# Rounding the attention and out-projection weights quarter by quarter from one queue

## The chip, the cores and the metric

The kernel runs on one core of a Trainium2 chip. The time is that of the device for one execution, in microseconds (us), the median of several runs. The engines are TensorE (PE in the rows; its weight loads are PEld), VectorE (DVE), ScalarE (ACT), GpSimd (POOL) and SyncE (SP), which issues almost all transfers (DMA). Every engine works through a queue of its own in order; engines wait for one another by semaphores.

## The reference: one hybrid decoder layer

The input is x, 1024 tokens of 1024 numbers, float32. In short:

```
h    = rms_norm(x, norm1_w)
proj = h @ w_in             # q, k, v of 4 attention heads; q, k, v, z, a, b of 4 DeltaNet heads
da_o = diff_attention(rms_norm(q), rms_norm(k), v, lam)    # (softmax(q1 k1^T) - lam softmax(q2 k2^T)) v, causal
da_o = rms_norm(da_o) * (1 - lam_init)
dn_o = gated_delta_rule(...)                               # in chunks of 64, from a causal convolution
x    = x + concat(da_o, dn_o) @ w_out                      # out-projection, 1024 x 1024
h    = rms_norm(x, norm2_w)
x    = x + relu(h @ w_up)^2 @ w_down                       # 1024 x 4096 and 4096 x 1024
```

## The kernel before

Every matrix operand is split into a rounded high part, made on ScalarE by a copy into the type fp32r, and a low part, the rest, subtracted on VectorE. A product is then three matmuls: high by high, low by high, high by low. For the normed activations the parts are `hH` and `hL`; for weights they are `wH` and `wL`, made from a raw tile `wraw` that a DMA fills.

The order of TensorE's instructions is fixed by a planner, the class `Interleave` (object `flow`). The parts of the kernel are generators ("streams") with a priority: a stream yields the planned time at which it may go on, and the planner, which keeps a clock of TensorE's planned work (`flow.now`) and planned queues of the other engines (`flow.chain`), takes the next ready stream and emits its instructions. The instructions of ScalarE, VectorE and SyncE are ordered behind that by a scheduler that goes by their emission order and what they depend on. So a planned time that is too early leads to an instruction that waits at the head of its engine's queue.

The stretch that matters here runs, in the profile, from about 300 to 670 us. In it work these streams, side by side:

- `da_units` (L802): six units, namely k, q and v of two head pairs. A unit is 256 columns of `w_in` for all 8 token tiles: 8 tiles of 24 matmuls of 128x256 (L824 to L826), each followed by a copy `qn` and, for q and k, a norm.
- `da_turns` (L781) transposes the normed q and k (L789, L790) and stores them in DRAM as `qa`, `qb` (`qk_d`).
- `scores` (L894) loads them back, multiplies (L944, L945, L947), takes the maximum (L949) and the exponential `pexp` (L953). `values` (L969) transposes the weights of attention (L980), copies them with ScalarE (`at`, L982), multiplies them with v (L992), copies the result (`om`, L997) and stores it (`mixa_d`).
- `mixed` (L1040) loads the mixed outputs back and turns them into `hH`, `hL` (`to_hT`, L239 to L245).
- `outproj` (L1065) multiplies by `w_out` in halves (L1079 to L1081), adds into `acc` (L1086), and begins the second norm in `norm2` (squares L1098, `nrt` L231, `nr` L232 on GpSimd, products `hn` L1105).
- `backs` (L1204) transposes the normed tiles (`turn_b`, L1181, L1182) and forms the operands of the MLP (`kept`, `T0h`, `T0l`, `hH`, `hL`), and `up_first` (L1257) does the first up-projection products (L1249 to L1251). The MLP uses a scheme of seven half-size products instead of eight; its weights go through `split` (L1166, copy L1168 and subtract L1169).

A unit's weights are four quarters of 256 KB. `load_unit` (L186) emits, for all four at once, the DMA (L198), the copy (L200) and the subtract (L201). There are only two buffers of `wraw`, so that quarters 3 and 4 can be loaded only after the subtracts of quarters 1 and 2. `da_units` and `outproj` call it when the unit before begins; `first_ops` (L1230) does likewise for the first up-projection weights, its second half emitted behind a product of the second norm (`normed_by`). `unit_time` (L656) gives the planned times at which the quarters are ready, by which the streams yield.

Of the kernel before, what the change touches and what calls it, by code (L numbers as in the profile page):

```python
# [18 lines left out]
P = 128  # L19
SEQ = 1024  # L20
DM = 1024
KB = DM // P
# [99 lines left out]
def tile_hymba_layer(  # L122
# [111 lines left out]
    def to_hT(src, tb, bank, k0=0, nk=KB, keep=None):  # L234
        sl = slice(tb * P, (tb + 1) * P)
        for g in range(0, nk, 4):
            ps = bank()
            for j in range(4):
                T.transpose(ps[:, j * P:(j + 1) * P], src[:, (g + j) * P:(g + j + 1) * P], ident)  # L239
# [4 lines left out]
            S.copy(hH[:, ks, sl], psv)  # L244
            V.tensor_tensor(hL[:, ks, sl], psv, hH[:, ks, sl].bitcast(F32), ALU.subtract)  # L245

    def normed(dst, src, wb, pool, parts=1):
        sq = pool.tile([P, DM], F32, tag="nsq", name="nsq", bufs=1)
# [407 lines left out]
    def unit_time(eng="V", rate=610.0):  # L656
# [3 lines left out]
            done.append(flow.chain(("S", 520.0), (eng, rate), start=start + DMA_T))  # L660
        return done

    def scan():
        St = {}
        psA = pA.tile([P, 512], F32, name="ps_A")
        PA = {h: psA[:, h * P:(h + 1) * P] for h in range(HEADS)}

        def load(c):
            pka = sb.tile([P, HEADS, 3, P], F32, tag="pka", name="pka", bufs=2)
            for h in range(HEADS):  # L670
                nc.sync.dma_start(pka[:, h], park_d[h, c, :, 0:3, :])
            return pka

        nxt = load(0)
        for c in range(NT):
# [126 lines left out]
    def da_units():  # L802
        todo = [(g, kind) for g in range(2) for kind in (1, 0, 2)]

        def unit_w(i):
            g, kind = todo[i]
            return load_unit(w_in_v, [(512 * kind + 256 * g, 256)]), unit_time()

        w = unit_w(0)
        freed = [0.0, 0.0]  # L810
        n = 0
        for i, (g, kind) in enumerate(todo):
            (wh, wl), wt = w
            for tb in range(NT):
                if tb == 0:
                    if i + 1 < len(todo):
                        w = unit_w(i + 1)
                    else:
                        pre.append((load_unit(w_out_v, [(0, 512)], 4, 4), unit_time()))
                sl = slice(tb * P, (tb + 1) * P)  # L820
                yield max(freed[n % 2], wt[0] if tb == 0 else 0.0), None
                ps = pj.tile([P, 512], F32, tag="pj", name="ps_qk")
                for k in range(KB):
                    T.matmul(ps[:, :256], hH[:, k, sl], wh[:, k, :], start=(k == 0), stop=False)  # L824
# [2 lines left out]
                    if k % 2 == 1:  # L827
                        flow.pe(6 * TR)
                        if k < KB - 1:
                            yield wt[k // 2 + 1], None  # L830
                while len(late) > 2:
                    yield flow.now + 50, None
                qn = sd.tile([P, 256], F32, tag="qn", name="qn", bufs=4)
                if kind == 2:
                    S.copy(qn, ps[:, :256])
# [4 lines left out]
                else:  # L840
                    sq = sd.tile([P, 256], F32, tag="qsq", name="qsq", bufs=1)
                    S.activation(sq, ps[:, :256], AF.Square)
                    S.copy(qn, ps[:, :256])
# [125 lines left out]
    def values():  # L969
        for _ in order:  # L970
# [4 lines left out]
            for g in range(0, tb + 1, 4):  # L975
# [3 lines left out]
                for j in range(ng):  # L979
                    T.transpose(pt[:, j * P:(j + 1) * P], pe[:, (g + j) * P:(g + j + 1) * P], ident)  # L980
                at = ap.tile([P, 512], F32, tag="at", name="at", bufs=2)
                S.copy(at[:, :ng * P], pt[:, :ng * P])  # L982
                ats.append(at)
                if g + 4 > tb:
                    ready.pop(0)
# [27 lines left out]

    def turn(src, t, tb, k0, keep=None):
        r = yield from flow.bank("px", at=t)
        to_hT(src, tb, lambda: bank_tile(px, r, "ps_tr"), k0, 4, keep)
# [48 lines left out]
    def outproj():  # L1065
# [5 lines left out]

        def half(kh, w, n, tb):
            sl = slice(tb * P, (tb + 1) * P)
            (wh, wl), wt = w
            r = yield from flow.bank("pf", at=wt[0])
            ps = bank_tile(pf, r, "ps_op")
            for k in range(4):
                kk = 4 * kh + k
# [2 lines left out]
                T.matmul(ps, hL[:, kk, sl], wh[:, k, :], start=False, stop=(k == 3))  # L1081
                flow.pe(648)
                if k < 3:
                    yield wt[k + 1], None
            a = accs[tb][:, 512 * n:512 * n + 512]
            V.tensor_tensor(a, a, ps, ALU.add)  # L1086
            t = flow.chain(vec(512))
# [3 lines left out]
        def norm2(tb, pos):  # L1091
# [10 lines left out]
            for i in range(2):  # L1102
                sl = slice(512 * i, 512 * i + 512)
                if i == 0 or pos >= 4:
                    normed_by[:] = [V.scalar_tensor_tensor(hn[i], accs[tb][:, sl], r, w2b[:, sl], ALU.mult, ALU.mult)]  # L1105
# [31 lines left out]
        while todo:  # L1137
# [22 lines left out]
            [P, 2, 512], F32, name="X1")  # L1160
        state["out"] = True

    normed_by, normed_at, held_back, banks, normed2, raws, kept, u, ups = [], {}, [], {}, set(), [], {}, {}, {}
    k1, k2, tok1, tok2 = slice(0, 4), slice(4, 8), slice(512, 1024), slice(0, 512)

    def split(dst, src):  # L1166
# [8 lines left out]
    def turn_b(hn, t, tb):  # L1175
        sl = slice(tb * P, (tb + 1) * P)
        for i in range(2):
            r = yield from flow.bank("px", at=t)
            p = bank_tile(px, r, "ps_tr")
            for j in range(4):  # L1180
                T.transpose(p[:, j * P:(j + 1) * P], hn[i][:, j * P:(j + 1) * P], ident)  # L1181
            S.copy(hn[i], p)  # L1182
            flow.pe(4 * TR)
            t = flow.chain(act(512))
            flow.hold(r, t)
# [43 lines left out]

    def first_ops(g):  # L1230

        ops = []
        for tag, ks in (("wH", k1), (("wL", "wH")[g], k2)):
            o = staged(tag)
            o = o[:, :2048].rearrange("p (a k c) -> p a k c", a=2, k=4)
            for p in range(2):
                raw = laid("wraw")[:, :512]
                raw = raw.rearrange("p (k c) -> p k c", k=4)
                cs = slice(p * P, p * P + P)
                nc.sync.dma_start(raw, w_up_v[:, ks, 512 * g + p * P:512 * g + p * P + P])  # L1240
                split((o[:, 0, :, cs], o[:, 1, :, cs]), raw)
            ops.append((o[:, 0], o[:, 1]))
        return ops

    def prod_up(ps, op, p, h, start, stop):

# [10 lines left out]
    def up_first():  # L1257
        while not state["free"] or len([d for d in normed_at if d < 4]) < 4 or "wu" not in pools:
            yield flow.now + 50, None
        wu, wt = pools["wu"]  # L1260
        yield max(normed_at[d] for d in range(4)), None
        for g in range(2):
            for i in range(2):
# [6 lines left out]
                        yield flow.now + 50, None  # L1270
                    bank = banks["Z"] = [bank_tile(px, ("px", p), f"Z{p}") for p in range(2)]
                for p in range(2):
                    yield wt[2 * i + p], None
                    for k in prod_up(bank[p], wu[i], p, H_OPS[i + 1], True, i == 1):
                        flow.pe(680)
                        if k < 3:
                            yield flow.now, None
                    if (g, i, p) == (0, 1, 0):
                        while not state["out"]:
                            yield flow.now + 50, None  # L1280
                        with tc.issue_after(normed_by[0].ins):
                            ahead = first_ops(1), unit_time()
            if g == 0:
                wu, wt = ahead

    def read_first():
        a0 = pools["uz"].tile([P, 2, 512], F32, tag="ua0", name="ua0")
# [335 lines left out]
```

## Time and profile before

| | |
|---|---|
| median of 3 runs | 1273.77 us (1269.63 to 1275.3) |
| the profiled execution | 1275.89 us, its span 1274.2 us |
| TensorE busy | 1230.6 us (97%) |
| VectorE, ScalarE, GpSimd busy | 827.6 us (65%), 596.8 us (47%), 146.2 us (11%) |
| mean granted TensorE clock | 0.992 |

In the rows that follow, a line such as L200 is a line of the kernel before; `x72` counts instructions; a bracket `[4.23 <-DMA wraw]` gives the idle time of that engine just before the instruction and what ended it. PEclk is the granted clock of TensorE as a share of the full one.

### The profile page before, as it was taken

The page shows a single profiled execution, that of the slowest core. Times are in us where ns is not written, and L with a number is a line of the kernel's source. Part 1 is how long each engine was busy: PE and PEld are TensorE (multiplying, and loading weights), DVE is VectorE, ACT ScalarE, POOL GpSimd, SP SyncE. Part 2 cuts the span into 40 slices and gives each one's busy share as a digit, 9 for nine tenths or more (in the row PEclk, how much of TensorE's full clock was granted, in tenths as well). Part 3 has the DMA queues.
Part 4 walks back from the last instruction along what each step waited for, and adds up shares of the span by engine and source line. Part 5 has one row for each costly group of instructions (what it writes and reads, how often), then busy time and mean ns, then how long its engine had stood idle before and what let it go on. Part 6 is the DMA issues. An engine that isn't in the chain of part 4 may idle for free.

```text
span 1274.2 us, 18904 instructions
## 1 busy us (share of the span) xinstructions
PE 1230.6 (97%) x6925; PEld 1061.7 (83%) x6925; DVE 827.6 (65%) x1412; ACT 596.8 (47%) x1173; POOL 146.2 (11%) x178
## 2 busy tenths in 40 slices
PE   6989999999998999999999999999999999999998
PEld 5968788899998997887788888888887788888887
DVE  6459888657646647776588656555566765677553
ACT  5335554334445545566567445544554333333331
POOL 2327411012212210001210000000000000000000
PEclk9989999999999999999999999999999999999999
DMA  7134464357849556433353645343368955422311
GB/s 251 41 83 122 115 177 125 89 182 221 281 144 248 159 170 178 96 95 107 122 182 129 218 166 178 136 164 127 122 215 304 356 198 195 169 99 100 122 44 67
DMA packets 165958, 200.55 MB, mean 157 GB/s; under 512 B 20921, under 2 KB 126185, under 8 KB 165865
## 3 DMA queue, kind: packets, MB, share of 16 engines
q1 hardware_dynamic: 165864, 199.34, 48.4%
q8 instruction: 55, 0.90, 0.3%
q14 instruction: 39, 0.31, 0.1%
HBM read 133.23 MB, written 66.06 MB: 156 GB/s over the span
## 4 chain that ended last, share of the span: by engine, by line
PE 84%; DMA 6%; DVE 5%; ACT 2%; issue 2%; SPq 1%; DVEq 0%; POOL 0%; ACTq 0%
PE X L1251 4%; PE X L1249 4%; PE X L1250 4%; PE X L1545 4%; PE X L1546 4%; PE X L1544 4%; PE ps_qk L824 3%; PE ps_qk L825 3%; PE ps_qk L826 3%; PE Y L1251 2%; PE Y L1249 2%; PE Y L1250 2%; DMA wraw<-in_w_in_dram 2%; PE ps_dn L206 2%; PE ps_o L992 2%; PE ps_dn L207 2%
## 5 line engine op out<-in xcount | busy, mean ns | idle before, releaser
L1168 ACT CAST hH<-ur 128x1024 fp32r<-128x1024 f32 x56 | 58.7, 1050 | 174.9 <-PE Z L1545 84.0
L1169 DVE TENSOR_TENSOR hL<-ur,hH 128x1024 fp32r<-128x1024 f32 x56 | 68.3, 1223 | 84.0 <-ACT hH L1168 84.0
L824 PE MATMUL ps_qk<-wH,hH 128*128 128x256 f32 x384 | 116.0, 302 | 0.0
L825 PE MATMUL ps_qk<-wL,hH 128*128 128x256 f32 x384 | 109.5, 285 | 0.0
L826 PE MATMUL ps_qk<-wH,hL 128*128 128x256 f32 x384 | 109.4, 285 | 0.0
L1169 DVE TENSOR_TENSOR op<-raw,op 128x1024 fp32r<-128x1024 f32 x48 | 58.7, 1223 | 74.2 <-PE X L1250 39.5
L1545 PE MATMUL X<-hL,hH 128*128 128x512 f32 x224 | 87.3, 390 | 2.1 <-DVE hL L1169 2.1
L1544 PE MATMUL X<-hH 128*128 128x512 f32 x224 | 87.3, 390 | 1.4 <-DVE b L1446 1.4
L1546 PE MATMUL X<-hH,hL 128*128 128x512 f32 x224 | 87.2, 389 | 0.0
L206 PE MATMUL ps_dn<-hH,wH 128*128 128x512 f32 x192 | 77.0, 401 | 4.9 <-ACT cp L441 4.9
L207 PE MATMUL ps_dn<-hL,wH 128*128 128x512 f32 x192 | 76.4, 398 | 0.0
L208 PE MATMUL ps_dn<-hH,wL 128*128 128x512 f32 x192 | 76.2, 397 | 0.0
L824 PEld LDWEIGHTS ps_qk<-wH,hH 128*128 128x128 f32 x384 | 74.5, 194 | 0.1
L825 PEld LDWEIGHTS ps_qk<-wL,hH 128*128 128x128 f32 x384 | 74.6, 194 | 0.0
L826 PEld LDWEIGHTS ps_qk<-wH,hL 128*128 128x128 f32 x384 | 74.2, 193 | 0.0
L201 DVE TENSOR_TENSOR wL<-wraw,wH 128x512 fp32r<-128x512 f32 (+1 forms) x72 | 50.4, 715 | 30.0 <-ACT wH L200 29.8
L200 ACT CAST wH<-wraw 128x512 fp32r<-128x512 f32 (+1 forms) x72 | 42.9, 620 | 57.3 <-DMA wraw<-in_w_in_dram 41.8
L1169 DVE TENSOR_TENSOR hL<-dw,hH 128x1024 fp32r<-128x1024 f32 x56 | 67.9, 1218 | 2.6 <-ACT hH L1168 2.6
L1168 ACT CAST op<-raw 128x1024 fp32r<-128x1024 f32 x48 | 50.4, 1052 | 36.9 <-PE Y L1251 19.9
L445 DVE SCALAR_TENSOR_TENSOR cy<-cp,pv,cy 128x512 f32<-128x512 f32 x72 | 59.4, 827 | 9.6 <-ACT cy L443 8.9
L1168 ACT CAST hH<-dw 128x1024 fp32r<-128x1024 f32 x56 | 58.4, 1047 | 12.4 <-PE Z L1546 8.1
L949 DVE TENSOR_REDUCE mx<-ps_sc 128x1 f32<-128x128 f32 (+7 forms) x64 | 47.7, 755 | 17.2 <-PE ps_sc L947 16.8
(340 smaller groups left out, 3457.8 us busy)
## 6 DMA issues: line engine op xcount, KB each, us to landing
ur<-ud SPq DMA_DIRECT2D x28, 1024.0 KB, 4.9
raw<-in_w_up_dram SPq DMA_DIRECT2D x32, 512.0 KB, 3.8
dw<-in_w_down_dram SPq DMA_DIRECT2D x32, 512.0 KB, 6.8
wraw<-in_w_in_dram SPq DMA_DIRECT2D x48, 256.0 KB, 3.2
qk_d<-qa SPq DMA_DIRECT2D x32, 256.0 KB, 3.6
ud<-ua SPq DMA_DIRECT2D x16, 512.0 KB, 4.2
ud<-s SPq DMA_DIRECT2D x16, 512.0 KB, 2.8
pka<-park_d SPq DMA_DIRECT2D x32, 192.0 KB, 4.2
```

What stands on the lines that cost most here:

```text
L206: T.matmul(ps, lh(k), rh(k), start=(k == 0), stop=False)
L207: T.matmul(ps, lh(k), rl(k), start=False, stop=False)
L824: T.matmul(ps[:, :256], hH[:, k, sl], wh[:, k, :], start=(k == 0), stop=False)
L825: T.matmul(ps[:, :256], hH[:, k, sl], wl[:, k, :], start=False, stop=False)
L826: T.matmul(ps[:, :256], hL[:, k, sl], wh[:, k, :], start=False, stop=(k == KB - 1))
L1168: S.copy(dst[0], src)
L1169: V.tensor_tensor(dst[1], src, dst[0].bitcast(F32), ALU.subtract)
L1249: T.matmul(ps, op[0][:, k, cs], h[0][:, k, :], start=start and k == 0, stop=False, skip_group_check=True)
L1250: T.matmul(ps, op[0][:, k, cs], h[1][:, k, :], start=False, stop=False, skip_group_check=True)
L1544: T.matmul(bank[t], v[0][:, j, sl], v[2][:, j], start=s0, stop=False, skip_group_check=True)
L1545: T.matmul(bank[t], v[0][:, j, sl], v[3][:, j], start=False, stop=False, skip_group_check=True)
L1546: T.matmul(bank[t], v[1][:, j, sl], v[2][:, j], start=False, stop=s1, skip_group_check=True)
```

## The change

The roundings of these weights are emitted by a stream of their own, `casts`, from one queue `wq`, a quarter at a time. A load is emitted by `load_part`: two at the start of the queue, and from then on one with each rounding that is emitted, if a unit with quarters left is queued. A quarter is due when the planner's clock has gone 300 ns beyond the assumed time of a load, `DMA_T` (2500 ns), from the load's emission; its copy is then emitted with an ordering edge behind the last ScalarE operation emitted (`state["act"]`, noted at the copies `qn`, `at`, `turn_b` and those of `to_hT`). The users wait by `part(w, i)`, quarter by quarter. `first_ops` returns a queue entry; its roundings may go on from the state "ready" or "out", and are no longer behind a product of the second norm.

```diff
+    def load_part(w):
+        i = len(w["raw"])
+        src, k = w["parts"][i][2:]
+        raw = laid("wraw")[:, :k * src.shape[-1]].rearrange("p (k c) -> p k c", k=k)
+        nc.sync.dma_start(raw, src)
+        w["raw"].append(raw)
+        w["due"].append(flow.now + DMA_T + 300.0)
+
+    def casts():
+        while "wu" not in pools or wq:
+            w = wq[0] if wq else None
+            if w is None or w["due"][len(w["at"])] > flow.now or not state.get(w["gate"], True):
+                yield flow.now + 50, None
+                continue
+            i = len(w["at"])
+            hi, lo = w["parts"][i][:2] if w["gate"] is None else w["ops"]()[i]
+            with tc.issue_after(state["act"].ins) if "act" in state else ExitStack():
+                S.copy(hi, w["raw"][i])
+            V.tensor_tensor(lo, w["raw"][i], hi.bitcast(F32), ALU.subtract)
+            w["at"].append(flow.chain(("S", 520.0), ("V", 610.0)))
+            if i == 3:
+                wq.pop(0)
+
+            nxt = next((v for v in wq if len(v["raw"]) < 4), None)
+            if nxt is not None:
+                load_part(nxt)
+            yield flow.now, None
+
+    def part(w, i):
+
+        while len(w["at"]) <= i:
+            yield flow.now + 50, None
+        yield w["at"][i], None
...
-            (wh, wl), wt = w
+            this, (wh, wl) = w, w["ops"]
             for tb in range(NT):
+                sl = slice(tb * P, (tb + 1) * P)
+                yield freed[n % 2], None
+                yield from part(this, 0)
                 if tb == 0:
-                    if i + 1 < len(todo):
-                        w = unit_w(i + 1)
-                    else:
-                        pre.append((load_unit(w_out_v, [(0, 512)], 4, 4), unit_time()))
-                sl = slice(tb * P, (tb + 1) * P)
-                yield max(freed[n % 2], wt[0] if tb == 0 else 0.0), None
+                    w = ahead_unit(*(unit_w(i + 1) if i + 1 < len(todo) else (w_out_v, [(0, 512)], 4, 4)))
+                    if i + 1 == len(todo):
+                        pre.append(w)
...
-                            yield wt[k // 2 + 1], None
+                            yield from part(this, k // 2 + 1)
...
-                S.copy(at[:, :ng * P], pt[:, :ng * P])
+                state["act"] = S.copy(at[:, :ng * P], pt[:, :ng * P])
...
-                    normed_by[:] = [V.scalar_tensor_tensor(hn[i], accs[tb][:, sl], r, w2b[:, sl], ALU.mult, ALU.mult)]
+                    V.scalar_tensor_tensor(hn[i], accs[tb][:, sl], r, w2b[:, sl], ALU.mult, ALU.mult)
...
-        w1 = load_unit(w_out_v, [(512, 512)], 4, 4), unit_time()
+        w1 = ahead_unit(w_out_v, [(512, 512)], 4, 4)
...
-            w = load_unit(w_out_v, [(512 * n, 512)], 0, 4), unit_time()
+            w = ahead_unit(w_out_v, [(512 * n, 512)], 0, 4)
...
-                    pools["wu"] = first_ops(0), unit_time()
+                    pools["wu"] = [first_ops(g) for g in range(2)]
...
-                    if (g, i, p) == (0, 1, 0):
-                        while not state["out"]:
-                            yield flow.now + 50, None
-                        with tc.issue_after(normed_by[0].ins):
-                            ahead = first_ops(1), unit_time()
-            if g == 0:
-                wu, wt = ahead
+            wu = pools["wu"][1]
...
+    flow.add(0.5, casts())
```

`ahead_unit` makes the tiles `wH`, `wL` and the list of four quarters, and `queued` puts them on the queue. The out-projection's `half` and `up_first` change their waits to `part` in the same way. Where a first-operand quarter lies depends on `halves`, which allots the tiles of the second half only when its first rounding is emitted.

More of the change, by code (lines that the diff above doesn't have):

```diff
@@ L243, in to_hT @@
                 S.copy(keep, psv)
-            S.copy(hH[:, ks, sl], psv)
+            last = S.copy(hH[:, ks, sl], psv)
             V.tensor_tensor(hL[:, ks, sl], psv, hH[:, ks, sl].bitcast(F32), ALU.subtract)
+        return last
     def normed(dst, src, wb, pool, parts=1):
@@ L661, in unit_time, with ahead_unit, queued @@
         return done
+    wq = []
+    def ahead_unit(src, ranges, k0=0, nk=KB):
+        width = sum(n for _, n in ranges)
+        st = 2 * UC // width
+        wh, wl = [staged(t)[:, :nk * width].rearrange("p (k c) -> p k c", k=nk) for t in ("wH", "wL")]
+        c0 = ranges[0][0]
+        parts = [(wh[:, k:k + st], wl[:, k:k + st], src[:, k0 + k:k0 + k + st, c0:c0 + width], st)
+                 for k in range(0, nk, st)]
+        return queued((wh, wl), parts)
+    def queued(ops, parts, gate=None):
+        w = {"ops": ops, "parts": parts, "gate": gate, "raw": [], "due": [], "at": []}
+        wq.append(w)
+        if len(wq) == 1:
+            load_part(w)
+            load_part(w)
+        return w
+    def load_part(w):
[27 more added lines that the diff above has]
+        yield w["at"][i], None
     def scan():
@@ L806, in unit_w @@
             g, kind = todo[i]
-            return load_unit(w_in_v, [(512 * kind + 256 * g, 256)]), unit_time()
-        w = unit_w(0)
+            return w_in_v, [(512 * kind + 256 * g, 256)]
+        w = {"ops": load_unit(*unit_w(0)), "at": unit_time()}
         freed = [0.0, 0.0]
@@ L834, in da_units @@
                 if kind == 2:
-                    S.copy(qn, ps[:, :256])
+                    state["act"] = S.copy(qn, ps[:, :256])
                     st = nc.sync.dma_start(v_d[g, tb], qn.rearrange("p (h e) -> p h e", h=2))
@@ L842, in da_units @@
                     S.activation(sq, ps[:, :256], AF.Square)
-                    S.copy(qn, ps[:, :256])
+                    state["act"] = S.copy(qn, ps[:, :256])
                     sn = sd.tile([P, 4], F32, tag="sn", name="sn", bufs=2)
@@ L1015, in turn @@
         r = yield from flow.bank("px", at=t)
-        to_hT(src, tb, lambda: bank_tile(px, r, "ps_tr"), k0, 4, keep)
+        state["act"] = to_hT(src, tb, lambda: bank_tile(px, r, "ps_tr"), k0, 4, keep)
         flow.pe(4 * TR)
@@ L1073, in half @@
             sl = slice(tb * P, (tb + 1) * P)
-            (wh, wl), wt = w
-            r = yield from flow.bank("pf", at=wt[0])
+            wh, wl = w["ops"]
+            yield from part(w, 0)
+            r = yield from flow.bank("pf")
             ps = bank_tile(pf, r, "ps_op")
@@ L1083, in half @@
                 if k < 3:
-                    yield wt[k + 1], None
+                    yield from part(w, k + 1)
             a = accs[tb][:, 512 * n:512 * n + 512]
@@ L1161, in outproj @@
         state["out"] = True
-    normed_by, normed_at, held_back, banks, normed2, raws, kept, u, ups = [], {}, [], {}, set(), [], {}, {}, {}
+    normed_at, held_back, banks, normed2, raws, kept, u, ups = {}, [], {}, set(), [], {}, {}, {}
     k1, k2, tok1, tok2 = slice(0, 4), slice(4, 8), slice(512, 1024), slice(0, 512)
@@ L1181, in turn_b @@
                 T.transpose(p[:, j * P:(j + 1) * P], hn[i][:, j * P:(j + 1) * P], ident)
-            S.copy(hn[i], p)
+            state["act"] = S.copy(hn[i], p)
             flow.pe(4 * TR)
@@ L1230, in first_ops, with halves @@
     def first_ops(g):
+        srcs = [w_up_v[:, ks, 512 * g + p * P:512 * g + p * P + P] for ks in (k1, k2) for p in range(2)]
         ops = []
[L1233 to L1243, printed above, removed]
+        def halves():
+            if not ops:
+                for tag in ("wH", ("wL", "wH")[g]):
+                    o = staged(tag)[:, :2048].rearrange("p (a k c) -> p a k c", a=2, k=4)
+                    ops.append((o[:, 0], o[:, 1]))
+            return [(o[0][:, :, p * P:p * P + P], o[1][:, :, p * P:p * P + P]) for o in ops for p in range(2)]
+        if g == 0:
+            halves()
+        w = queued(halves, [(None, None, src, 4) for src in srcs], ("ready", "out")[g])
+        w["halves"] = ops
+        return w
     def prod_up(ps, op, p, h, start, stop):
@@ L1259, in up_first @@
             yield flow.now + 50, None
-        wu, wt = pools["wu"]
+        wu = pools["wu"][0]
         yield max(normed_at[d] for d in range(4)), None
@@ L1272, in up_first @@
                 for p in range(2):
-                    yield wt[2 * i + p], None
-                    for k in prod_up(bank[p], wu[i], p, H_OPS[i + 1], True, i == 1):
+                    yield from part(wu, 2 * i + p)
+                    for k in prod_up(bank[p], wu["halves"][i], p, H_OPS[i + 1], True, i == 1):
                         flow.pe(680)
```

## The prediction

> **What bounds the kernel now.** I read the summary first, then TensorE's waits over the stretch whose order the change moves (300 to 700 us), then the rows of the rounding copies and the timelines around the two longest waits.
>
> ```profile
> span 1274.2 us, 18904 instructions
> PE 1230.6 (97%) x6925; PEld 1061.7 (83%) x6925; DVE 827.6 (65%) x1412; ACT 596.8 (47%) x1173; POOL 146.2 (11%) x178
> PE 84%; DMA 6%; DVE 5%; ACT 2%; issue 2%; SPq 1%; DVEq 0%; POOL 0%; ACTq 0%
> L200 ACT CAST wH<-wraw 128x512 fp32r<-128x512 f32 (+1 forms) x72 | 42.9, 620 | 57.3 <-DMA wraw<-in_w_in_dram 41.8
> ```
>
> TensorE is busy in 97% of the span, so what a change of order can bring is idle time and lost clock of TensorE, nothing else. The copy that rounds a weight quarter (L200) costs 0.62 us, and ScalarE stands idle ahead of these copies mostly for the load of the raw weights. ScalarE is busy 47% and can afford to wait; what it must not do is wait with somebody's work behind it. The waits of TensorE in the moved stretch:
>
> ```profile
> PE ps_qkt L789 <- ACT at L982: 3.7, 1, 3.7
> PE ps_tr L239 <- DMA mt<-mixa_d: 2.3, 2, 1.4
> PE ps_at L980 <- ACT om L997: 2.2, 1, 2.2
> PE ps_at L980 <- DVE hL L245: 1.5, 1, 1.5
> PE ps_sc L945 <- DMA qb<-qk_d: 1.3, 1, 1.3
> PE ps_o L992 <- ACT at L982: 1.0, 1, 1.0
> PE ps_qkt L789 <- DVE qn L849: 0.9, 1, 0.9
> PE ps_sc L944 <- ACT pexp L953: 0.8, 1, 0.8
> PE ps_qkt L789 <- ACT om L997: 0.7, 1, 0.7
> PE ps_qkt L789 <- ACT osq L745: 0.2, 1, 0.2
> ```
>
> The columns are us in total, times, longest. None names a weight, but the timeline of ScalarE shows what stood ahead of the named copies (start, duration, and in brackets the idle time before and its releaser):
>
> ```profile
> 409.35 0.20 ACT L953 ACTIVATION_READ_ACCUMULATOR pexp<-ps_sc,mx 128x1 f32 x1
> 413.78 0.62 ACT L200 CAST wH<-wraw 128x512 fp32r<-128x512 f32 x1 [4.23 <-DMA wraw<-in_w_in_dram]
> 414.31 0.26 ACT L982 COPY at<-ps_at 128x128 f32<-128x128 f32 x1
> ...
> 541.27 0.62 ACT L200 CAST wH<-wraw 128x512 fp32r<-128x512 f32 x1 [2.74 <-DMA wraw<-in_w_out_dram]
> 542.68 0.25 ACT L997 COPY om<-ps_o 128x128 f32<-128x128 f32 x1
> ```
>
> The third quarter's rounding waits 4.23 us for its load at the head of ScalarE's in-order queue, and the attention copy that TensorE wants stands behind it. Over the stretch:
>
> ```profile
> DMA wraw<-in_w_in_dram: 15.2, 7
> DMA wraw<-in_w_out_dram: 8.8, 4
> ```
>
> ScalarE waited eleven times, 24 us, at these copies; eight TensorE waits stand behind such a copy or the subtract after it, 3.7 + 2.2 + 1.5 + 1.0 + 0.9 + 0.8 + 0.7 + 0.2 = 11.0 us. The cause is that a unit's four loads and roundings are emitted together and only two raw buffers exist, so loads 3 and 4 start after subtracts 1 and 2, while their copies already stand in ScalarE's queue.
>
> **What the stalls cost beside their length.** TensorE's timeline and the table by windows (PE, PEld, DVE, ACT, POOL busy, then PEclk):
>
> ```profile
> 414.62 0.47 PE L789 MATMUL ps_qkt<-ident,qn 128*128 128x128 f32 x1 [3.75 <-ACT at L982]
> 415.32 0.41 PE L825 MATMUL ps_qk<-wL,hH 128*128 128x256 f32 x1
> 415.53 0.41 PE L826 MATMUL ps_qk<-wH,hL 128*128 128x256 f32 x1
> ...
> 415.00:420.00 5.00, 5.00 (x26) 5.00 (x25) 3.29 (x9) 1.99 (x6) 1.01 (x1) 0.51 0.61 176
> 540.00:545.00 5.00, 2.75 (x12) 1.96 (x11) 2.45 (x3) 3.43 (x9) 0.00 (x0) 0.78 0.48 136
> 545.00:550.00 5.00, 5.00 (x23) 4.12 (x23) 3.67 (x9) 1.97 (x4) 0.55 (x1) 0.88 0.36 103
> ```
>
> After the gap of 3.75 us the granted clock is 0.51 for 5 us: 5 x 0.49 = 2.4 us lost. After that of 2.25 us the loss is 5 x 0.22 + 5 x 0.12 = 1.7 us. No other gap of the stretch shows a dip, the longest of them 1.5 us. Together 4.1 us.
>
> [...]
>
> **The change, part by part.** No engine gets more instructions; copies, subtracts and loads change places between about 300 and 670 us, and the order is as before from there on.
>
> *Attention and out-projection quarters.* Each copy now is emitted when its load is planned to have landed, pinned behind the last ScalarE work emitted, and the next load is issued with it. What counts is the TensorE work between the event that lets a load start and the first matmul that needs the rounded quarter (the cover), counted in the instruction order at the steps of rows like those above. Before, the covers of the quarters 3 and 4 are 4.8 to 9.7 us, and 4.8, 4.9 and 5.3 gave the gaps of 1.0, 2.25 and 3.75. The need, by the chain of waits, is
>
> ```profile
> 408.34 5.42 DMA wraw<-in_w_in_dram
> 413.78 0.62 ACT wH L200
> ...
> 536.96 4.28 DMA wraw<-in_w_out_dram
> ...
> 599.64 3.63 DMA wraw<-in_w_out_dram
> ```
>
> 3.6 to 5.4 us of load, 0.6 of copy, 0.6 of subtract, and small waits, 5.8 to 9.9 by stage (an estimate from cover plus stall). After the change the covers are 7.6 to 18.3; only the second attention unit has 6.8 where it may need 9.5. There I take 1.5 us left (bounds 0 and 2.7), 0.5 for all others (0 and 3, if ScalarE stands at some pinned copies as it does now). So -11.0 -4.1 + 2.0 = -13.1 us.
>
> *Loads beside them.* SP's queue gets the raw loads one by one between the other loads, instead of four in a row; the covers of the qb loads rise from 4.8 to 5.9 us, so the 1.3 us at qb should go (0 to 1.3), and of the 2.3 at mixa_d I take 1.0 (0 to 2.3), as one of its three covers stays at 4.9. Sum -2.3.
>
> *First up-projection operands.* They come through the same queue and no longer hang behind the second norm's product. No wait of TensorE in this stretch before is theirs, covers stay about 10 us: 0, hidden by the out-projection's matmuls (without them a load and copy, some 5 us).
>
> *The second norm.* This is where the change can lose. VectorE in 650 to 660 us:
>
> ```profile
> 650.00:655.00 5.00, 5.00 (x25) 4.10 (x25) 5.00 (x11) 3.56 (x8) 0.00 (x0) 1.00 0.86 269
> 655.00:660.00 5.00, 5.00 (x25) 4.09 (x24) 5.00 (x11) 3.01 (x6) 0.86 (x1) 1.00 0.71 224
> 655.00 0.69 DVE L1198 TENSOR_TENSOR hL<-hn,hH 128x512 fp32r<-128x512 f32 x1
> 655.60 0.68 DVE L1086 TENSOR_TENSOR acc<-acc,ps_op 128x512 f32<-128x512 f32 x1
> ...
> 658.74 1.41 DVE L1105 SCALAR_TENSOR_TENSOR hn<-acc,nr,w2b 128x512 f32<-128x512 f32 x2
> 660.06 0.15 DVE L231 TENSOR_SCALAR nrt<-nss 128x1 f32<-128x1 f32 x1
> 659.87 0.60 PE L1181 MATMUL ps_tr<-ident,hn 128*128 128x128 f32 x4
> 664.22 0.60 PE L1181 MATMUL ps_tr<-ident,hn 128*128 128x128 f32 x4
> ```
>
> VectorE is full for 10 us and TensorE yet has no gap, because first up products lie ahead of the last transposes (659.87 and 664.22). In the changed order these transposes stand some 4 us of TensorE work earlier, and VectorE's work ahead of them is not less: between its last prerequisite and its transposes the seventh tile has 1.1 us of cover, the eighth 0.7. Walked with the steps above (0.60 us a tensor operation, 1.32 the pair of products): the seventh tile needs the sum (0.60) and the pair (1.32) with a handover, about 2.6 against 1.1, so 1.5 us of gap; the eighth has 11 tensor operations, small ones (0.2) and the pair behind the seventh, 11 x 0.60 + 0.2 + 1.32 = 8.1 us against some 4.8 us of TensorE work, so 3.3 us. Sum +4.8 (bounds 0, if VectorE arrives with work done earlier, and 6.5, if ScalarE's squares are late too). A gap of 3.3 lies between the two that cost 2.4 and 1.7 of clock: +2.0 (0 to 4.1). So +6.8.
>
> [...]
>
> **Sum.** -13.1 - 2.3 + 6.8 = -8.6 us. Against the profiled execution (1275.89 us: its span and 1.7 around it) that is 1267.3. That execution lies 2.1 us above the median of the runs, 1273.77, whose spread is 5.7 us, so I place the new median at 1266, some 0.6% lower. 0.5% (6.4 us) is about what a measurement of this kernel tells from no change.
>
> **Rivals.**
> *Norm covered, the whole gain kept.* VectorE may reach the zone with its queue emptier, since no gap of TensorE delays what it is handed. Against it: the order of its queue, in which subtracts and sums stand ahead of the products. -13.1 - 2.3 = -15.4: about 1259.
> *The gain is eaten.* The weight waits go, but the second unit costs its 2.7, the others 3, the norm 6.5 with 4.1 of clock, qb and mixa_d give nothing: -15.1 + 5.7 + 10.6 = +1.2 at worst, half way to it -4: about 1271.
> *The copies still block (slower; it doesn't do what it says).* The pin only says behind what a copy stands, not that its load has landed: the planner's due is 2.8 us after issue, and the rows above show loads of 3.6 to 5.4. If loads are late against the plan, each copy waits up to 2.6 us at the head of ScalarE's queue, now in the midst of attention work. For it: the two long gaps came from just such copies. Against: the covers. A gap of 2.2 with 1.7 of clock costs 3.9; the gains of 15.4 less 6.8 at the norm are used up by 3 such gaps among the 11 waits, and with 5 it is 1266 + 5 x 3.9 = 1286, slower. It decides from four on (1282).
>
> **How the numbers follow.** Forecast 0.45 (1262 to 1270), whole gain 0.15, eaten 0.2, blocking copies 0.2. Of the forecast about two thirds lies under 1267.4, with the whole gain 0.45 x 0.67 + 0.15 = 0.45 faster; the remainder of the forecast and the eaten gain, with some of the blocking case that lands within, 0.34 same; 0.21 slower. The range reaches from the whole gain to a blocking case with four gaps: 1258 to 1283.
>
> **What would show it.** Right: no ScalarE wait over 1.5 us ahead of a weight copy, the gaps near 414 and 543 us and their dips gone, a gap of about 3 us ahead of the last norm transposes with VectorE full. Wrong: waits behind weight copies at other places, a norm zone without a gap, or gaps at loads (qb, mixa_d) that were covered.

## The result and the profile after

The changed kernel takes 1277.74 us (median of 12 runs, 1276.65 to 1280.66), the kernel before, in the same rounds, 1270.11 us (1266.16 to 1276.32): a ratio of 1.0052, 95% interval 1.0035 to 1.007 (the ratio on record; that of the two medians is 1.0060, inside this interval). It is slower by half a per cent; forecast was a gain of 0.6%. The profiled execution after is of 1280.06 us, that before of 1275.89, a difference of 4.2 us; both lie above their medians, the one before by 5.8 us.

The summary of the changed kernel, its TensorE waits in the moved stretch, and the waits of ScalarE at its weight copies (L701 now):

```profile
span 1278.4 us, 18923 instructions
PE 1233.2 (96%) x6925; PEld 1061.2 (83%) x6925; DVE 827.8 (65%) x1412; ACT 596.3 (47%) x1173; POOL 146.7 (11%) x178
```

```profile
PE ps_tr L1237 <- DVE hn L1161: 5.0, 3, 3.2
PE ps_o L1047 <- ACT at L1037: 3.6, 2, 2.9
PE ps_tr L239 <- DVE wL L702: 1.9, 1, 1.9
PE ps_A L757 <- ACT sy L748: 1.8, 2, 1.0
PE ps_qkt L844 <- ACT om L1052: 1.3, 1, 1.3
PE ps_sc L1000 <- DMA qb<-qk_d: 1.1, 1, 1.1
PE ps_tr L239 <- DMA mt<-mixa_d: 1.0, 1, 1.0
PE ps_A L734 <- DVE S L763: 0.7, 1, 0.7
PE ps_sc L999 <- ACT pexp L1008: 0.6, 1, 0.6
PE ps_tr L239 <- DMA mt<-mixn_d: 0.4, 1, 0.4
```

```profile
DMA wraw<-in_w_in_dram: 9.5, 7
DMA wraw<-in_w_out_dram: 6.7, 5
DMA wraw<-in_w_up_dram: 2.5, 4
```

The first row is the second norm, forecast at 4.8 us. The rest, 12.7 us with two waits too short for the table, is the attention stretch, which was forecast nearly empty. At the copies of `w_in` and `w_out` ScalarE still waits 16.2 us, against 24 before; the 2.5 us at `w_up` are those of the first operands, whose copies waited 5.0 us before (at L1168). The loads between 300 and 610 us, in KB and median us from issue to landing, took longer than the 2.8 us after which a copy is due:

```profile
wraw<-in_w_in_dram SPq DMA_DIRECT2D x14, 256.0 KB, 4.4
wraw<-in_w_out_dram SPq DMA_DIRECT2D x16, 256.0 KB, 3.5
```

Two pieces of ScalarE's timeline, and a row of VectorE's, show what stands behind these copies:

```profile
383.65 0.19 ACT L1008 ACTIVATION_READ_ACCUMULATOR pexp<-ps_sc,mx 128x1 f32 x1
387.06 0.62 ACT L701 CAST wH<-wraw 128x512 fp32r<-128x512 f32 x1 [3.22 <-DMA wraw<-in_w_in_dram]
387.59 0.47 ACT L848 ACTIVATE qa<-ps_qkt,pv 128x256 fp32r<-128x256 f32 x1
388.21 0.62 ACT L701 CAST wH<-wraw 128x512 fp32r<-128x512 f32 x1 [0.15 <-DMA wraw<-in_w_in_dram]
...
389.20 0.26 ACT L1037 COPY at<-ps_at 128x128 f32<-128x128 f32 x1
...
492.63 0.62 ACT L701 CAST wH<-wraw 128x512 fp32r<-128x512 f32 x1 [2.87 <-DMA wraw<-in_w_out_dram]
...
493.29 1.49 DVE L702 TENSOR_TENSOR wL<-wraw,wH 128x512 fp32r<-128x512 f32 x2 [2.17 <-ACT wH L701]
```

At 383.8 us ScalarE comes to a copy whose load lands only at 387; the copy `at` that TensorE needs for ps_o stands behind it, a gap of 2.9 us. At 489.8 us ScalarE waits in the same way for an out-projection quarter; here VectorE waits for the copy with its subtract `wL`, and the profile puts a wait of TensorE's transposes down to that subtract (1.9 us). It is the picture of before at other places. The clock, by windows of the changed kernel:

```profile
390.00:395.00 5.00, 4.71 (x23) 3.66 (x22) 3.41 (x12) 2.70 (x10) 1.72 (x2) 0.66 0.84 230
495.00:500.00 5.00, 4.57 (x19) 3.65 (x18) 4.41 (x10) 1.91 (x6) 0.55 (x1) 0.66 0.66 215
660.00:665.00 5.00, 3.15 (x12) 2.67 (x13) 4.77 (x8) 2.44 (x5) 0.00 (x0) 0.80 0.28 81
665.00:670.00 5.00, 5.00 (x22) 4.09 (x22) 3.03 (x4) 1.01 (x2) 0.00 (x0) 0.86 0.08 28
1010.00:1015.00 5.00, 3.75 (x10) 2.99 (x11) 5.00 (x8) 1.99 (x2) 0.00 (x0) 0.66 1.02 409
```

Both gaps are followed by a dip of 5 x 0.34 = 1.7 us, the norm's 3.2-us gap by 5 x 0.20 + 5 x 0.14 = 1.7 us.

Setting equal TensorE work of the two profiles side by side, the changed kernel's start was 2.1 us shorter (no edit lies there), it gains some 2.3 us between 300 and 650 us, loses some 7.0 at the second norm, and 1.6 more by a dip at 1010 us that the first profile doesn't have: -2.1 - 2.3 + 7.0 + 1.6 = +4.2. The split at 650 us is good to about 1 us only, as the order differs there; the sum of the two terms, +4.7, can be read from the same matmuls on both sides.

### The profile page after: what moved, and what is told of

Same layout as the page of the kernel before. It is cut to its first block, busy times and chain, and to the rows that moved or that the text cites. A ratio compares the mean times of both kernels' runs of the same rounds, so it can differ in the third digit from the quotient of the medians.

```text
span 1278.4 us, 18923 instructions
## 1 busy us (share of the span) xinstructions
PE 1233.2 (96%) x6925; PEld 1061.2 (83%) x6925; DVE 827.8 (65%) x1412; ACT 596.3 (47%) x1173; POOL 146.7 (11%) x178
## 4 chain that ended last, share of the span: by engine, by line
PE 81%; DMA 7%; DVE 6%; ACT 2%; issue 2%; SPq 1%; POOL 0%; DVEq 0%; POOLq 0%; ACTq 0%
PE X L1309 4%; PE X L1310 4%; PE X L1311 4%; PE X L1600 4%; PE X L1601 4%; PE X L1599 4%; DMA wraw<-in_w_in_dram 3%; PE ps_qk L879 3%; PE ps_qk L880 3%; PE ps_qk L881 3%; PE Y L1309 2%; PE Y L1310 2%; PE Y L1311 2%; PE ps_o L1047 2%; PE ps_dn L206 2%; PE ps_dn L207 2%
## 5 line engine op out<-in xcount | busy, mean ns | idle before, releaser
L1224 ACT CAST hH<-dw 128x1024 fp32r<-128x1024 f32 x56 | 58.4, 1047 | 13.1 <-PE Z L1601 8.0
L1008 ACT ACTIVATE pexp<-ps_sc,mx 128x128 f32<-128x128 f32 (+7 forms) x64 | 47.3, 741 | 25.6 <-DVE mx L1004 25.4
L1004 DVE TENSOR_REDUCE mx<-ps_sc 128x1 f32<-128x128 f32 (+7 forms) x64 | 47.5, 753 | 13.1 <-PE ps_sc L1002 12.7
L1135 PE MATMUL ps_op<-wH,hH 128*128 128x512 f32 x128 | 55.3, 432 | 0.0
```

The source lines that it names most:

```text
L1224: S.copy(dst[0], src)
```

## The experiments

Theory 1, made from these views: two separate losses. Copies still wait for loads that take longer than the plan's 2.8 us, which takes back most of the gain in the attention stretch, and the re-ordering costs some 7 us at the norm. Rivals: one part of the change alone does it; or the gaps come from the traffic or from too much work on ScalarE. Ratios are to the kernel before in the same rounds.

**The parts alone.** units_only queues the quarters of the units and the out-projection, with the first operands as before:

```diff
-                    pools["wu"] = [first_ops(g) for g in range(2)]
+                    pools["wu"] = first_ops(0), unit_time()
```

(with `first_ops`, `up_first` and `normed_by` as before). first_only is the reverse: `load_unit` and `unit_time` for units and out-projection, the queue for the first operands.

> The quarters of the attention units and of the out-projection come through the queue as in the changed kernel; the first up-projection operands are rounded as before (all four at once, the second half behind a product of the second norm). Theory 1 (two separate losses: gaps behind weight copies that still wait for slow loads, about 9 us of TensorE waits between 310 and 604 us, and some 7 us at the second norm, both from the re-ordering): the attention stretch stays as in the changed kernel; the norm's transposes stand later in the order than there, but still closer together than before, so the norm's gaps fall from 5.0 to 1 to 3 us, and the time to 1272 to 1276. Theory 2 (the first operands alone cost it, the units gain): norm gaps under 0.5 us and a time at or under that of before, 1266 to 1270. Theory 3 (the units alone cost it): norm gaps as in the changed kernel and 1277 to 1279.

> Only the first up-projection operands come through the queue; attention units and out-projection round their quarters as before. Theory 1: the gaps near 408, 414 and 543 us are those of before; the transposes of the seventh and eighth norm tile stand some 3 us of TensorE work earlier than before, which gives 2 to 4 us of gap there, and 1272 to 1275. Theory 2: the full norm loss, 5 us of gap and its clock, 1277. Theory 3: no loss, 1270.

units_only: ratio 0.999 (0.9976 to 1.0004). Its gap at the norm is 0.7 us, less than theory 1 said; between 300 and 610 us it keeps 12.4 us of gaps. So the units' part neither gains nor loses. first_only: 1.0034 (1.0018 to 1.0049), at the upper end of what theory 1 said, with this row of TensorE's waits:

```profile
PE ps_tr L1236 <- DVE hn L1160: 3.2, 1, 3.2
```

The parts make -0.1% and +0.34%, together +0.52%: they don't add up, because both move the norm's transposes. The norm's loss comes with the first operands; with the units' re-ordering its gaps grow from 3.2 to 5.0 us. (In clock first_only's profile loses more there, a granted clock of 0.90 from 650 to 680 us or 30 x 0.10 = 3.0 us, than the changed kernel's 1.7.)

**The norm.** late_turns plans the last four norm tiles 3 us later, norm_relief takes half of their products off VectorE:

```diff
-                return hn, flow.chain(vec(512, 60), vec(512, 60), start=t - flow.HOP)
+                return hn, flow.chain(vec(512, 60), vec(512, 60), start=t - flow.HOP) + 3000.0
```
```diff
-                if i == 0 or pos >= 4:
+                if i == 0:
```

> The changed kernel with the last four norm tiles planned 3 us later, so that TensorE's order has more of the first products ahead of their transposes (the sixth tile 3.5 us of work later, the seventh 3.5, the eighth 2.8). If the place of the transposes is the whole cause, the norm's gaps fall from 5.0 to under 1 us and the clock dip at 660 to 670 us goes: 1270 to 1272. If VectorE only falls further behind and the gap moves, it stays at 3 us or more and 1275 to 1278.

> The changed kernel with the second half of the product hn of the last four norm tiles made by ScalarE and GpSimd instead of VectorE (the form that the first four tiles have), TensorE's order unchanged. If a full VectorE makes the transposes wait (the prediction's walk), each of these tiles needs 0.67 us less of it and the gaps ahead of the norm's transposes fall from 5.0 to 1 to 2.5 us, without a clock dip: 1271 to 1274. If squares or GpSimd's power are late, the gaps stay at 4 us or more, 1277.

late_turns: 0.9998 (0.9982 to 1.0014); the norm's gaps fall from 5.0 to 0.9 us and the dip there is gone. The place of the transposes is the cause. Not all of the 0.54% between the two kernels need be the norm's: in late_turns' profile the gaps between 300 and 610 us are 9.3 us instead of 12.7, with one dip instead of two, though TensorE's order is the same up to 640 us. norm_relief: 1.0029 (1.0013 to 1.0045), between the two answers (TensorE's waits again):

```profile
PE ps_tr L1237 <- DVE hn L1161: 2.4, 1, 2.4
...
PE ps_tr L1237 <- POOL hn L1164: 1.4, 1, 1.4
...
PE ps_tr L1237 <- ACT hn L1238: 0.3, 1, 0.3
```

The wait for VectorE halves, and GpSimd's product (1.35 us in the median in the changed kernel's profile, where VectorE's takes 0.74) is late instead, 4.2 us in all, without a dip. A full VectorE is what the transposes met, but the half that ScalarE and GpSimd took over was late there too.

**The weight copies' wait.** no_wait lets the copies and subtracts of these quarters read a resident tile; no_loads drops their loads besides. Both compute other products: they leave out the use of these weights, with every copy, subtract and matmul in place.

```diff
+            raw = w["raw"][i]
+            if w["gate"] is None:
+                n = hi.shape[-2] * hi.shape[-1] // P
+                raw = ident.unsqueeze(1).to_broadcast([P, n, P])
...
-                S.copy(hi, w["raw"][i])
-            V.tensor_tensor(lo, w["raw"][i], hi.bitcast(F32), ALU.subtract)
+                S.copy(hi, raw)
+            V.tensor_tensor(lo, raw, hi.bitcast(F32), ALU.subtract)
```

> The changed kernel, but the copies and subtracts of the attention and out-projection quarters read a resident tile, not the loaded one; the loads are still issued. It computes other products, so it leaves out the use of these weights; every instruction is there. If copies that wait for their loads at the head of ScalarE's queue are the cause of the gaps in the attention stretch, the gaps ahead of the scan's products (2.5 us), at 389 (2.9), 428 (1.3) and 495 us (1.9) go with two dips of 1.6 us each, and the time is 1266 to 1269; the norm's 5 us of gaps stay. If these gaps come from the traffic or from ScalarE's load, they stay or move to other loads and the time is 1274 to 1278.

> As the run before it, without the loads of these quarters (36 DMAs of 256 KB left out). Against it this shows what the loads' traffic costs the other loads: if nothing, the same time within 1 us; if the gaps at qb (1.1 us) and mixa_d (1.0 us) and slow stores hang on it, 2 to 4 us less, 1263 to 1266.

no_wait: 1.0083 (1.0063 to 1.0103), slower than either answer. Its gaps between 300 and 610 us did go, from 12.7 to 3.5 us, without a dip there. But nothing tied the loads to the copies any more; SyncE got them all early, ahead of the loads of `gb` in the scan's preparation. Its timeline (a row counts a run of DMAs) and TensorE's waits from 250 to 300 us:

```profile
241.21 10.12 SPq L688 DMA_DIRECT2D wraw<-in_w_in_dram  x7
251.43 2.78 SPq L571 DMA_DIRECT2D gb<-fsg_d  x6
```
```profile
PE ps_p L577 <- DMA gb<-fsg_d: 5.5, 1, 5.5
PE ps_h L585 <- DVE W L589: 5.2, 1, 5.2
```

In the changed kernel that stretch has no wait, and six of the `gb` loads are issued at 241. So its total tells nothing about theory 1. no_loads has no such queue: 0.9973 (0.9959 to 0.9987), 1265.37 us, gaps of 3.2 us between 300 and 610, while the norm's 4.5 us are still there. Against the changed kernel's 1.0052 that is 0.8% or 10 us for waits and loads together. The two kernels agree on what remains of the gaps, but neither has a load of these quarters in this stretch: no_wait issues its last one at 291 us. So some 9 of the 12.7 us go with the waits and this traffic together, and these two runs don't say how much is the wait's alone; that rests on the timelines above and on the due time below. They do show that it isn't the amount of work on ScalarE, which is unchanged.

**The due time.** late_due and units_late_due set the due of a quarter to 5.8 us after its load:

```diff
-        w["due"].append(flow.now + DMA_T + 300.0)
+        w["due"].append(flow.now + DMA_T + 3300.0)
```

> The changed kernel with each quarter's rounding due 5.8 us after its load's emission instead of 2.8. If loads that take longer than the plan assumes make the copies wait at the head of ScalarE's queue (theory 1), ScalarE's waits ahead of the weight copies fall from 18.7 us to under 6 and TensorE's gaps between 310 and 604 us from 12.7 to under 5 us. The norm's transposes move further ahead in the order, so its gaps stay at 5 us or grow to 8. Time 1269 to 1275. If the waits have another cause (order of the other loads, ScalarE too busy), the gaps stay and the time is 1277 to 1280.

> units_only with the roundings due 5.8 us after their load's emission. In this kernel TensorE's order at the second norm is that of the kernel before (a whole group of first products ahead of the last transposes). Theory 1: both losses gone, TensorE's gaps between 310 and 670 us under 5 us against 14.9 before, no norm gap, and 1262 to 1266, faster than both. If late roundings only move the waits to TensorE (covers too short for a due of 5.8 us), gaps at the first matmuls of the units of 1 to 2 us each and 1268 to 1274.

Both miss: 1.0123 (1.01 to 1.0146) and 1.005 (1.0031 to 1.007), with gaps of 11.6 and 9.1 us between 300 and 610. In late_due ScalarE's waits at weight copies fall, to 10.8 us, but the next load is issued with a rounding, so all loads come later, and other transfers are now what is waited for (its TensorE waits, and a row of ScalarE's timeline):

```profile
PE ps_A L757 <- ACT sy L748: 5.8, 1, 5.8
PE ps_tr L1237 <- DVE hn L1161: 4.6, 1, 4.6
PE ps_tr L239 <- DMA mt<-mixa_d: 4.0, 2, 3.6
PE ps_sc L999 <- DMA qa<-qk_d: 3.4, 2, 3.1
...
339.30 0.47 ACT L848 ACTIVATE qa<-ps_qkt,qw 128x256 fp32r<-128x256 f32 x1 [6.63 <-DMA qk_d<-qa]
```

The longest gap is the same fault with a store: the copy `sy` stands in ScalarE's queue behind a copy `qa` that waits 6.63 us for the store of an earlier `qa`. That the moved weight loads made this store late is likely, but not shown. units_late_due has the first, third and fourth of these waits at 5.4, 3.8 and 2.9 us, and no gap at the norm, as expected from its order. The next runs ask whether a smaller delay does better, first on top of late_turns and further below without it.

> late_turns (ratio 0.9998, gaps of 0.9 us at the norm and 9.3 us between 300 and 610 us) with the roundings due 0.8 us later. If the loads' delay against the plan is what is left, ScalarE's waits at the copies lose up to 0.8 us each and TensorE's gaps fall to 5 to 7 us, ratio 0.995 to 0.998. If a later rounding only moves the waits, as the due of 5.8 us did, 0.999 to 1.004.

> The same with 1.5 us. If it helps as far as covers allow, 3 to 5 us of gaps left, ratio 0.993 to 0.997; if the next loads, issued with the later roundings, are now what is late, gaps of 2 us or more at qa, qb or the scan's copies and ratio 1.000 to 1.006.

turns_due800 (+0.8 us): 1.001 (0.9995 to 1.0026), no gain. ScalarE's waits for `w_in` and `w_out` fall from late_turns' 15.2 to 8.5 us, but TensorE's gaps stay (9.2 us), with 2.3 us now at loads of `pkb`. turns_due1500 (+1.5 us): 0.9966 (0.9951 to 0.9981), faster than both kernels. Its gaps between 300 and 610 us are 5.2 us (5.9 with one at 269), but both have a new one that late_turns lacks, where VectorE's backlog meets the next products (2.4 us in the latter).

> The changed kernel with the roundings due 1.5 us later and nothing else. If the two losses are separate, TensorE's gaps between 300 and 610 us are those of turns_due1500 (5.9 us against 12.7), the norm's transposes, which stand up to 2 us of work later than in the changed kernel, keep 2 to 4 us of its gaps, and the ratio is 0.999 to 1.002. If the due does nothing without the shift of the norm tiles, 1.004 to 1.007.

> units_only (first operands as in the kernel before, ratio 0.999, norm gap 0.7 us) with the roundings due 1.5 us later. If its remaining 11 us of gaps come from loads that are late against the plan, they fall to about 6, and the ratio is 0.993 to 0.996. If the first operands' place in the queue mattered for the attention stretch, 0.998 to 1.001.

> turns_due1500 (ratio 0.9966) with the last four norm tiles planned 1.5 us later instead of 3. If the shift of 3 us pushes VectorE's backlog into the next products (the gap of 2.4 us at 667 us, waiting for VectorE), that gap goes below 1 us with at most 1.5 us of gap at the transposes, ratio 0.993 to 0.997. If VectorE is simply short in this stretch, the sum of gaps between 640 and 680 us stays at 2.5 us or more, 0.996 to 0.999.

due1500 is the changed kernel with `DMA_T + 1800.0` in the line above and nothing else: 1264.8 us, 0.9955 (0.9937 to 0.9972), better than expected. From 1.0052 to 0.9955 is 1% or 12 us by one constant, which also changes the order of TensorE from 273 us on. Its TensorE waits, and ScalarE's at the copies:

```profile
PE ps_tr L1237 <- DVE hn L1161: 2.1, 1, 2.1
PE ps_o L1047 <- ACT at L1037: 1.6, 1, 1.6
PE ps_qkt L844 <- DVE qn L904: 1.4, 1, 1.4
PE ps_o L786 <- DMA pkb<-park_d: 0.9, 1, 0.9
PE ps_at L1035 <- ACT om L1052: 0.9, 1, 0.9
```
```profile
DMA wraw<-in_w_up_dram: 4.5, 6
DMA wraw<-in_w_in_dram: 3.3, 2
DMA wraw<-in_w_out_dram: 3.2, 3
```

The waits for w_in and w_out at the copies fall from 16.2 to 6.5 us, the gaps in the attention stretch from 12.7 to 5.4 (another 0.6, at `pexp`, is not in the rows above), the norm's from 5.0 to 2.1, and no dip lies in the moved stretch. units_due1500 has the lowest time of all, though not clear of due1500's, 1262.51 us, 0.9935 (0.9917 to 0.9953), as it was expected: gaps of 6.2 us in the attention stretch and 0.7 at the norm, as its first operands are rounded as before. due1500_t1500: 0.9958 (0.9944 to 0.9972); a gap of 1.8 us stays at the transposes, the one at 667 us is gone. On top of the later due the shift of the norm tiles brings nothing.

One profile of a kernel is a coarse measure, and these runs show how coarse. The changed kernel, units_only, norm_relief, late_turns and no_pin (below) have the same order of TensorE up to 640 us and the due of 2.8 us: their gaps between 300 and 610 us are 12.7, 12.4, 12.4, 9.3 and 13.4 us. The four with the due of 4.3 us have one order up to 635 us: 5.4, 6.2, 5.2 and 6.5. So a difference of 3 us between two profiles can be chance here; the two groups, though, don't overlap.

**The edge, and a second look at before.** no_pin drops the ordering edge; before_again is the kernel before.

```diff
-            with tc.issue_after(state["act"].ins) if "act" in state else ExitStack():
-                S.copy(hi, w["raw"][i])
+            S.copy(hi, w["raw"][i])
```

> The changed kernel without the ordering edge of the weight copies behind the last ScalarE operation emitted; TensorE's order is the same. If the edge keeps the copies from standing too early in ScalarE's queue, ScalarE's waits ahead of them grow from 18.7 us to over 24 and TensorE's gaps between 300 and 610 us from 12.7 to 15 or more, 1280 to 1285 by the scale of the changed kernel's 1277.7 against 1270.1 (ratio 1.007 to 1.012). If the loads alone decide it, the waits only change places and the time is that of the changed kernel, ratio 1.003 to 1.007.

> The kernel before, once more, for a second profile. If the half clock behind its gaps of 2.25 and 3.75 us follows from their length, it stands there again (2.4 and 1.7 us). If it hangs on where a gap falls, as the same gap of 2.05 us at about 1010 us suggests (a dip in three profiles of ten), one or both dips are missing and the execution is 2 to 4 us shorter than the first profile's 1275.9. Ratio 0.998 to 1.002.

no_pin: 1.0044 (1.003 to 1.0058), the changed kernel's own. ScalarE's waits at the copies do grow, to 23.9 us, but TensorE's gaps between 300 and 610 us only to 13.4. The edge isn't what costs or saves. before_again: 1.0004 (0.9987 to 1.0022), with both long gaps and both dips there again; its profiled execution took 1273.47 us, 2.4 less than the first. The gaps of this second profile at 408 and 536 us are 2.6 and 2.8 us, and by these windows their dips cost 5 x (0.21 + 0.14) and 5 x (0.24 + 0.11), 1.75 us each:

```profile
405.00:410.00 5.00, 2.44 (x14) 2.24 (x14) 1.72 (x6) 1.80 (x5) 0.00 (x0) 0.79 0.91 247
410.00:415.00 5.00, 5.00 (x38) 4.98 (x37) 2.60 (x7) 2.28 (x8) 1.01 (x1) 0.86 0.68 189
535.00:540.00 5.00, 3.83 (x15) 3.16 (x16) 3.45 (x6) 3.87 (x11) 0.55 (x1) 0.76 0.34 94
540.00:545.00 5.00, 5.00 (x31) 4.31 (x31) 3.21 (x7) 1.02 (x3) 0.00 (x0) 0.89 0.30 92
```

## Why the prediction was wrong

*What bounds the kernel* was read rightly: the gaps behind weight copies are there in both profiles of before, and no_loads and units_due1500, with gaps of 3.2 and 6.2 us, show that most of them can be had back.

*Attention and out-projection quarters, -13.1 us: this step failed.* Its sum left 2.0 us for gaps behind weight copies. The changed kernel has there gaps of 0.8 + 1.0 + 2.9 + 1.3 + 1.9 + 0.7 = 8.6 us and 3.4 us of clock, 12.0 in all: the saving of this step is 15.1 - 12.0 = 3.1 us instead of 13.1. The covers were counted from a load to the first matmul that needs the rounded quarter, and those did suffice, for no gap waits for a quarter of its own. But the timeline quoted in the prediction showed that the victims are other copies in ScalarE's queue. For them the cover is from the load to the moment at which ScalarE comes to the copy, and the change sets that at 2.8 us of planned time, while the prediction itself quoted loads of 3.6 to 5.4. The numbers stood in the rival of the blocking copies, which gave them a chance of 0.2. Its mechanism is what happened, with two gaps of its price and four small ones. due1500 shows that this due was what the change had mis-set: 1.5 us more takes the gaps from 12.7 to 5.4. As it moves the loads and TensorE's order too, how much of this is the wait alone is not shown.

*Loads beside them, -2.3:* qb went from 1.3 to 1.1 and mixa_d from 2.3 to 1.0, so -1.5. The sum is about right by luck: qb kept nearly all of its wait, mixa_d lost more than forecast, and in norm_relief, with the same order, mixa_d has 2.0 again. Small other waits (0.7 for the scan's state, 0.6 for `pexp`, 0.4 at mixn_d and two of 0.1) were not forecast.

*First operands, 0:* no wait for them appeared, but first_only shows that queueing them moves the norm's transposes and costs 0.34%. The prediction had that loss in its next step, as one of the order, without the edit that causes it.

*The second norm, +6.8:* right. Gaps 5.0 against 4.8, the largest 3.2 against 3.3, with VectorE busy 4.77 of the 5 us around it, and late_turns confirms the place of the transposes as the cause. The clock, 1.7 against 2.0, came out by luck: the gap of 3.18 us in no_loads stayed without a dip (last section).

*The sum:* with the measured terms it is -3.1 - 1.5 + 6.7 and 2.0 of small waits that were not counted, +4.1 us, against the -2.3 + 7.0 that the two profiles show. The base was too high besides: 1273.77 from three runs became 1270.11 with twelve, and the prediction's 1266 - (-8.6) stands for a base of 1274.6, so that a right difference would still have been given some 4.5 us too long.

## What to carry to other kernels

Where a copy waits for a load in an in-order queue, count the cover for what stands behind the copy, not for who needs its result: a rounding that is due before its load has landed blocks strangers, as the wait of 3.22 us at 387 us held up `at` and left TensorE a gap of 2.9 us. An assumed load time in a planner is worth measuring at the stretch where it is used; here 1.5 us on it decided between 0.5% lost and 0.45% gained; 0.8 us, tried with late_turns, gained nothing, and 3 us overshot. When a re-ordering lets one engine's work come earlier, look at the engine that feeds it, and if that is full over the stretch (VectorE here 4.77 of 5 us), the time gained ahead can come back as a gap there (5.0 us here).

## What the runs showed of the hardware

The length of a gap of TensorE alone does not tell whether clock is lost behind it. One gap in the down-projection part, at about 1010 us, is 2.05 us long in 14 of the 17 profiles; a dip follows it in 4 of them (the row at 1010 to 1015 above is one) and not in the other 10: over the 5 us that begin 1 us before the gap ends, the granted clock is 0.66 to 0.70 in the four and 1.00 in the ten. The norm's gap of 3.17 us in the changed kernel was followed by a dip, that of 3.18 us in no_loads was not.

Between 300 and 1015 us the changed kernel has four dips, which begin at 389.95, 495.76, 663.01 and 1011.17 us; each lasts 3.41 us at a granted clock of 0.50. The windows below stand around the norm's gap in the changed kernel, then, behind TensorE's row of that gap, in no_loads. In the changed kernel TensorE is idle for 2.2 of the 3.4 us ahead of the dip; in no_loads it is idle for 3.2 of 5 us and the clock stays at 1.00:

```profile
659.60:663.01 3.41, 1.17 (x8) 1.07 (x9) 3.41 (x7) 2.19 (x5) 0.01 (x1) 1.00 0.03 10
663.01:666.43 3.42, 3.42 (x12) 2.73 (x11) 2.07 (x4) 0.70 (x2) 0.00 (x0) 0.50 0.50 153
...
644.73 0.63 PE L1244 MATMUL ps_tr<-ident,hn 128*128 128x128 f32 x4 [3.18 <-DVE hn L1168]
...
640.00:645.00 5.00, 1.82 (x12) 1.26 (x11) 4.77 (x9) 3.38 (x6) 0.55 (x1) 1.00 0.46 142
645.00:650.00 5.00, 5.00 (x27) 4.16 (x26) 3.79 (x6) 1.69 (x3) 0.00 (x0) 1.00 0.33 105
650.00:655.00 5.00, 5.00 (x24) 4.13 (x23) 3.87 (x7) 3.00 (x4) 0.00 (x0) 1.00 0.00 0
```

Elsewhere a dip came with less: in turns_due1500 TensorE is idle for 1.55 of the 5 us from 325 us, and the granted clock falls to 0.94 there and to 0.72 in the 5 us after. What decides whether a dip follows is not shown.

So a forecast of a dip behind a gap of 2 to 3 us is a chance; that this is part of why the kernel before spreads over 10 us is likely, but not shown.
